# Eight modulation blocks a layer in 128-column pieces, issued ahead of the attention

## The chip, the cores and the metric

The kernel runs on one core of a Trainium2 chip. The metric is device time of one launch in microseconds (us). Matrix products run on TensorE (PE), which has two clock levels, 1.2 and 2.4 GHz; the profile gives the granted clock as a share of the higher one. VectorE (DVE), ScalarE (ACT) and GpSimd (POOL) do the rest. Each engine executes its own instructions in the order in which the build put them. Most loads and stores are issued from SP's queue, some from POOL's and ACT's.

## What is computed

One step of a two-layer trunk over 512 latent and 128 context tokens of 1024 channels. The parts that matter here:

```
for each layer l:
  m = silu(cond) @ w_mod[l] + b_mod[l]        # cond: latent c and context c_ctx; 6 * 1024 columns
  shift1, scale1, gate1, shift2, scale2, gate2 = six slices of m
  h = rms(x) * (1 + scale1) + shift1
  z = h @ w_in                                # columns for scan, queries, keys/values, gMLP
  y_a = two-way diagonal scan (16 groups, 64 complex states), GLU
  y_b = attention, 8 heads, queries and keys out of compressed vectors
  y_c = gMLP over chunks of 128 tokens
  x = x + gate1 * (concat(rms(y_a), rms(y_b), rms(y_c)) * g) @ w_out
  h = rms(x) * (1 + scale2) + shift2
  x = x + gate2 * (silu(conv3(h @ up_gate)) * conv3(h @ up_value)) @ w_down
```

Both condition vectors together are two rows, so the modulation is a product of two rows with a 1024 x 6144 matrix: 24 MB of weights a layer for little arithmetic.

## The kernel before

The activations lie transposed, channels on the partitions, 642 token columns in two halves. Products with large weights are made of three single-pass matmuls of high and low parts (`mm3`, lines 139 to 143); the parts come from `wload` (line 120), which loads 512 KB into one of three shared "raw" buffers, copies it to the high part on ACT and subtracts on DVE (`split`, line 115).

The 12 modulation blocks of 512 columns of a layer are made by the generator `mod_blocks` (line 230). Blocks 0 to 3 (shift1, scale1) come before the layer; blocks 4 to 11 are needed from the output projection on (`update`, line 1490, and the second norm). One step of the generator loads two of the eight k-tiles of a block (256 rows of 512 columns, runs of 2 KB) into a raw buffer on SP's queue (line 256) and issues two matmuls (line 260): the stationary operand is `sT`, 32 columns for a k-tile, the moving one 512 columns of float32, and the output lies in one of four groups of 32 partitions, k modulo 4. After four steps ACT copies the bank to `modev`, and with the next block's first step four transposes, a DVE reduce over the four groups, an add of the bias and at times a third operation give the columns (`finish`, line 235). The bank comes from the pool `pz` (two banks, tag "z"), which the attention uses for its transposes. One layer's generator of blocks 4 to 11 has 33 steps.

`mixers` (line 830) receives that generator as `fill`. Its order in the code: scan inputs and token-major parts of `w_in`, gMLP; in layer 0 then the scan tables of four quarters (`ssm_tables`, line 529, stores on SP's queue) and the scans (`ssm_quarter`, line 697, whose loads of tables are on POOL's queue); in layer 1 the scans come earlier, their tables having been made before. Then the compressed queries and keys (three column tiles of `w_in`, two halves each, `in_half` at line 854), keys and values (`w_ukv`, line 1019), queries (`w_uq`, line 1037). Five steps of `fill` are issued there, at line 1057. Then `attention` (line 1182): the context's own attention, and four passes of two heads each. `maxima` (line 1232) is a generator with a step for each query tile, and a step of `fill` is issued after each: eight in the context part, then eight in each of the passes 0 to 2 as far as there are any; what is left is issued at line 1420.

The build schedules ahead: it walks the instructions with an estimate of their times and priorities that follow the order of the code, gives out the buffers of a tag as they come free, and fixes the order on each engine. So an instruction may stand in its engine's queue before or after its neighbours in the code, but at run time each engine is in order.

PSUM in this part: two banks of `pz`, two of the pool `pa` (tag "a"; scores, statistics, token tiles) and two pairs of `pb`.

Of the kernel before, what the change touches and what calls it, by code (L numbers as in the profile page):

```python
# [10 lines left out]
F32 = mybir.dt.float32  # L11
# [17 lines left out]
NS = 82           # scan slots per row  # L29
# [18 lines left out]
class Trunk:  # L48
# [17 lines left out]
    def banks(self, pairs):  # L66
        """PSUM of one phase: six banks, as four single ones or two pairs of them."""
# [30 lines left out]
    def rsqrt(self, v, n):  # L98
        """v: [128, n] tile -> tile of 1/sqrt(v)."""
# [15 lines left out]
    def split(self, raw, hi, lo):  # L115
        """hi + lo == raw, each short enough for one float32r pass."""
        self.nc.scalar.copy(hi, raw)  # L117
        self.nc.vector.tensor_tensor(lo, raw, hi.bitcast(F32), op=OP.subtract)  # L118

    def wload(self, src, shape, pool=None, tags=("whi", "wlo"), bufs=5, into=None):  # L120
        """src: DRAM AP [128, a, b] (a*b <= 1024), or a list of (first index in a, AP)
        -> (hi, lo) views of that shape."""
        a, b = shape
        raw = self.wp.tile([128, 1024], F32, name=self.uid("raw"), tag="raw", bufs=3)
# [41 lines left out]
    def params(self, l):  # L166
        """Vectors of layer l with their index on the partitions."""
# [48 lines left out]
    def cond(self):  # L216
        """silu of both condition vectors, as 32-column stationary blocks."""
# [12 lines left out]
    def mod_blocks(self, l, blocks):  # L230
        """Blocks of 512 columns of the modulation of layer l; a generator of four steps a
        block and a last one."""
        nc = self.nc

        def finish(b, ev):
            pt = self.pz("modt")
            for i in range(4):
                self.tr(pt[:, i * 128:(i + 1) * 128], ev[:, i * 128:(i + 1) * 128])
            red = self.smt([128, 4, 2], "modred")
            nc.vector.tensor_reduce(  # L240
                red, pt.rearrange("p (i q r) -> p i r q", i=4, q=4)[:, :, 0:2, :],
                axis=AX.X, op=OP.add)
            m = self.mod[l][:, 4 * b:4 * b + 4, :]
            bias = self.prm[l][:, 4 * b:4 * b + 4]
            nc.vector.tensor_tensor(m, red, bc(bias[:, :, None], [128, 4, 2]), op=OP.add)
            if b // 2 in (1, 4):
                nc.vector.tensor_scalar(m, m, 1.0, None, op0=OP.add)

        last = None
        for b in blocks:  # L250
            src = self.I["w_mod"][l, :, b * 512:(b + 1) * 512].rearrange("(k p) n -> p k n", p=128)
            ps = self.pz("mod")
            for kp in range(4):
                raw = self.wp.tile([128, 1024], F32, name=self.uid("raw"), tag="raw", bufs=3)
# [16 lines left out]

    def modcol(self, l, i, k, c):
        return self.mod[l][:, i * 8 + k, c:c + 1]

    # ---------------------------------------------------------------- residual in and out
    def load_x(self):
# [3 lines left out]
        for tt in range(5):  # L280
            raw = self.wp.tile([128, 1024], F32, name=self.uid("raw"), tag="raw", bufs=3)
# [9 lines left out]
    def store_x(self, tiles):  # L291
        nc, O = self.nc, self.O
        for tt in tiles:
            o = self.wp.tile([128, 1024], F32, name=self.uid("xo"), tag="raw", bufs=3)
# [25 lines left out]
    def norm_stats(self, pool, lo, hi):  # L320
        """1 / rms of the columns lo .. hi, for bcast."""
# [39 lines left out]
    def bcast(self, pool, r, cols, *outs):  # L361
        """r: [128 tokens, n]; PSUM [128, 128] at column cols[i] of outs (512 columns each)
# [1385 lines left out]
```

## Time and profile before

| | us |
|---|---|
| runs shown, median (lowest to highest) | 1854.93 (1848.2 to 1855.78) |
| profiled execution, span | 1844.3 |
| PE busy in it | 1712.1 |
| DVE, ACT, POOL busy in it | 1153.7, 680.5, 265.3 |

The span runs from the first to the last instruction of one profiled execution. Busy times of an engine are unions over its instructions; matmuls are pipelined and overlap in the records. A float32 matmul leaves two records. A stretch below is given in us from the span's start.

### The profile page before, as it was taken

The page shows a single profiled execution, that of the slowest core. Times are in us where ns is not written, and L with a number is a line of the kernel's source. Part 1 is how long each engine was busy: PE and PEld are TensorE (multiplying, and loading weights), DVE is VectorE, ACT ScalarE, POOL GpSimd, SP SyncE. Part 2 cuts the span into 40 slices and gives each one's busy share as a digit, 9 for nine tenths or more (in the row PEclk, how much of TensorE's full clock was granted, in tenths as well). Part 3 has the DMA queues.
Part 4 walks back from the last instruction along what each step waited for, and adds up shares of the span by engine and source line. Part 5 has one row for each costly group of instructions (what it writes and reads, how often), then busy time and mean ns, then how long its engine had stood idle before and what let it go on. Part 6 is the DMA issues. An engine that isn't in the chain of part 4 may idle for free.

```text
span 1844.3 us, 28301 instructions
## 1 busy us (share of the span) xinstructions
PE 1712.1 (93%) x10864; PEld 1497.3 (81%) x10864; DVE 1153.7 (63%) x2461; ACT 680.5 (37%) x1210; POOL 265.3 (14%) x720
## 2 busy tenths in 40 slices
PE   6777889999999999999999988999989999999998
PEld 2665754559799899999998875455979999999998
DVE  5867784667764546466567578566777464655564
ACT  3342453532451414234244355353335132332241
POOL 3920300000024040439000120000000000000000
PEclk7886989999999999999999978999989999999999
DMA  7464534402433424134121633440222131321221
GB/s 222 135 163 123 140 110 159 138 1 69 126 119 100 151 65 126 54 98 125 54 89 66 159 107 105 156 141 1 69 69 92 32 107 44 94 82 45 81 81 58
DMA packets 201895, 182.44 MB, mean 99 GB/s; under 512 B 33438, under 2 KB 162780, under 8 KB 201760
## 3 DMA queue, kind: packets, MB, share of 16 engines
q1 hardware_dynamic: 182224, 163.57, 29.3%
q0 software_dynamic: 5104, 14.62, 2.7%
q10 hardware_dynamic: 14432, 2.44, 0.7%
q8 instruction: 86, 1.41, 0.3%
q14 instruction: 49, 0.40, 0.1%
HBM read 161.94 MB, written 18.64 MB: 98 GB/s over the span
## 4 chain that ended last, share of the span: by engine, by line
PE 74%; DVE 9%; DMA 8%; ACT 4%; POOL 3%; issue 2%; ACTq 0%; SPq 0%; DVEq 0%; POOLq 0%
PE up L141 11%; PE up L143 11%; PE up L142 11%; PE dn L142 5%; PE dn L141 5%; PE dn L143 5%; PE mod L260 4%; DMA raw<-w_mod 3%; PE o L1278 3%; PE wo L141 1%; PE wo L143 1%; PE wo L142 1%; PE s L1258 1%; PE mx L1239 1%; PE win L141 1%
## 5 line engine op out<-in xcount | busy, mean ns | idle before, releaser
L141 PE MATMUL up<-hh,whi 128*128 128x322 f32 x1408 | 436.5, 315 | 9.5 <-ACT hh L356 8.7
L142 PE MATMUL up<-hl,whi 128*128 128x322 f32 x1408 | 439.6, 313 | 2.1 <-DVE hl L357 1.9
L143 PE MATMUL up<-hh,wlo 128*128 128x322 f32 x1408 | 440.6, 314 | 0.4 <-DVE wlo L118 0.4
L141 PEld LDWEIGHTS up<-hh,whi 128*128 128x128 f32 x1408 | 266.2, 191 | 22.3 <-issue 11.0
L142 PEld LDWEIGHTS up<-hl,whi 128*128 128x128 f32 x1408 | 268.5, 191 | 2.9 <-DVE hl L357 2.9
L143 PEld LDWEIGHTS up<-hh,wlo 128*128 128x128 f32 x1408 | 267.9, 190 | 1.7 <-issue 1.0
L118 DVE TENSOR_TENSOR wlo<-raw,whi 128x1024 fp32r<-128x1024 f32 (+1 forms) x116 | 143.5, 1240 | 142.1 <-ACT whi L117 133.4
L142 PE MATMUL dn<-glo,dh 128*128 128x322 f32 (+1 forms) x704 | 217.7, 311 | 0.0
L143 PE MATMUL dn<-gh,dl 128*128 128x322 f32 (+1 forms) x704 | 217.4, 310 | 0.0
L141 PE MATMUL dn<-gh,dh 128*128 128x322 f32 (+1 forms) x704 | 208.8, 310 | 0.1
L1492 DVE SCALAR_TENSOR_TENSOR xT<-dn,mod,xT 128x320 f32<-128x320 f32 (+2 forms) x288 | 112.1, 435 | 129.9 <-PE dn L143 129.7
L117 ACT CAST whi<-raw 128x1024 fp32r<-128x1024 f32 (+1 forms) x116 | 120.4, 1041 | 157.1 <-PE up L142 63.9
L1523 ACT ACTIVATE cv<-up,prm,cw 128x321 f32<-128x321 f32 x88 | 54.2, 620 | 247.0 <-PE up L143 243.3
L143 PEld LDWEIGHTS dn<-gh,dl 128*128 128x128 f32 x704 | 132.9, 189 | 0.0
L142 PEld LDWEIGHTS dn<-glo,dh 128*128 128x128 f32 x704 | 132.7, 188 | 0.0
L141 PEld LDWEIGHTS dn<-gh,dh 128*128 128x128 f32 x704 | 130.3, 189 | 0.6 <-ACT gh L117 0.6
L260 PE MATMUL mod<-raw,sT 128*32 128x512 f32 x384 | 93.9, 672 | 20.1 <-DMA raw<-w_mod 17.2
L1524 DVE SCALAR_TENSOR_TENSOR cv<-up,cw,cv 128x320 f32<-128x320 f32 x88 | 48.3, 549 | 73.2 <-ACT cv L1523 73.0
L118 DVE TENSOR_TENSOR dl<-raw,dh 128x1024 fp32r<-128x1024 f32 x44 | 56.6, 1286 | 35.3 <-ACT dh L117 35.2
L1241 DVE TENSOR_REDUCE nml<-mx 128x1 f32<-128x640 f32 x64 | 51.1, 818 | 26.3 <-PE mx L1239 26.0
L117 ACT CAST dh<-raw 128x1024 fp32r<-128x1024 f32 x44 | 46.2, 1049 | 48.3 <-DMA raw<-ffn_w_down 44.9
L141 PE MATMUL wo<-yh,whi 128*128 128x322 f32 (+1 forms) x192 | 59.9, 317 | 1.8 <-ACT yh L117 1.0
(468 smaller groups left out, 3316.0 us busy)
## 6 DMA issues: line engine op xcount, KB each, us to landing
raw<-w_mod SPq DMA_DIRECT2D x96, 512.0 KB, 4.0
raw<-ffn_w_up SPq DMA_DIRECT2D x88, 512.0 KB, 4.0
raw<-ffn_w_down SPq DMA_DIRECT2D x44, 512.0 KB, 3.3
raw<-w_in SPq DMA_DIRECT2D x10, 512.0 KB, 4.8
WEd<-we SPq DMA_DIRECT2D x16, 256.0 KB, 2.1
Qd<-Q SPq DMA_DIRECT2D x32, 128.0 KB, 1.9
we<-WEd POOLq DMA_DIRECT2D x8, 512.0 KB, 4.1
qt<-Qd POOLq DMA_DIRECT2D x8, 512.0 KB, 5.0
```

The lines of the kernel that those rows point to most:

```text
L117: self.nc.scalar.copy(hi, raw)
L118: self.nc.vector.tensor_tensor(lo, raw, hi.bitcast(F32), op=OP.subtract)
L141: mm(ps, wh, xh, start=start, stop=False)
L142: mm(ps, wh, xl, start=False, stop=False)
L143: mm(ps, wl, xh, start=False, stop=stop)
L260: nc.tensor.matmul(ps[c:c + 32, :], self.sT[:, k, :], rv[:, j, :], start=k < 4, stop=k >= 4)
L1239: mm(pb[:, o, :320], qh[i][:96, tt * 128:(tt + 1) * 128], kh[i][:96, o * 320:(o + 1) * 320], start=True, stop=True)
L1241: V.tensor_reduce(nm[:, tt:tt + 1], pb[:, :, :320], axis=AX.XY, op=OP.max, negate=True)
L1278: mm(pb[i * 64:(i + 1) * 64, 0], Vt[:, kt, 2 * p + i], Ps[i][kt], start=kt == 0, stop=kt == 4)
L1492: self.nc.vector.scalar_tensor_tensor(self.xT[:, m, a:b], po[:, a - lo:b - lo], self.modcol(l, gi, m, c), self.xT[:, m, a:b], op0=OP.mult, ...
L1523: A.activation(z[:, 0:321], po[:, 0:321], AF.Identity, bias=b, scale=c1)
L1524: V.scalar_tensor_tensor(z[:, 1:321], po[:, 0:320], c0, z[:, 1:321], op0=OP.mult, op1=OP.add)
```

## The change

`mod_fill` takes the place of `mod_blocks` for blocks 4 to 11. One step loads all eight k-tiles of 128 columns (128 columns make runs of 512 B) into one raw buffer, issues eight matmuls of 128 columns, and ACT copies these 128 columns to `modev`; the fourth step of a block also does the transposes and the reduce at once. Banks come from `pa`. There are 32 steps a layer. They are issued two after the gMLP, two after each quarter of the scan tables (layer 0 only), two after each of six halves of the compressed projections, four after the key norms, and one after each of five query tiles: 31 in layer 0 and 23 in layer 1. The rest is issued by the loops of the attention, which are unchanged. `RAW` is 3, as before, and the loops over `range(0)` issue nothing. Comments and document strings are gone from the file, which has no effect.

```diff
     def mod_blocks(self, l, blocks):
...
+    def mod_fill(self, l, blocks):
+        nc = self.nc
+        def finish(b, ev):
+            pt = self.pa("modt")
+            for i in range(4):
+                self.tr(pt[:, i * 128:(i + 1) * 128], ev[:, i * 128:(i + 1) * 128])
+            self.mod_out(l, b, pt)
+        for b in blocks:
+            ev = self.smt([128, 512], "modev", bufs=1)
+            for i in range(4):
+                raw = self.wp.tile([128, 1024], F32, name=self.uid("raw"), tag="raw", bufs=RAW)
+                rv = raw.rearrange("p (k n) -> p k n", k=KT)
+                c = b * 512 + i * 128
+                nc.sync.dma_start(out=rv, in_=self.I["w_mod"][l, :, c:c + 128]
+                                  .rearrange("(k p) n -> p k n", p=128))
+                ps = self.pa("mod")
+                for k in range(KT):
+                    r = (k % 4) * 32
+                    nc.tensor.matmul(ps[r:r + 32, :128], self.sT[:, k, :], rv[:, k, :],
+                                     start=k < 4, stop=k >= 4)
+                nc.scalar.copy(ev[:, i * 128:(i + 1) * 128], ps[:, :128])
+                if i == 3:
+                    finish(b, ev)
+                yield
+    def mod_out(self, l, b, pt):      # reduce, bias, + 1: as in finish of mod_blocks
...
         self.gmlp(l, win, v, ssv, sq, yc, ssc)
+        for _ in range(2):
+            next(fill, None)
...
                 self.ssm_tables(0, q, tb, V)
+                for _ in range(2):
+                    next(fill, None)
...
                 in_half(m, w, s, put_c)
+                for _ in range(2):
+                    next(fill, None)
...
         self.key_norms(pt, ks, sc, ms, krn, kg)
+        for _ in range(4):
+            next(fill, None)
...
             V.tensor_reduce(ms[:, tt * 8:tt * 8 + 8], s2, axis=AX.X, op=OP.add)
+            for _ in range(1):
+                next(fill, None)
...
         self.query_norms(l, pt, qs, sc, ms, tab, [0, 1, 2, 3])
-        for _ in range(5):
-            next(fill, None)
...
-                fh, fl, second = self.mixers(l, M, n1, N, hh, hl, self.mod_blocks(l, range(4, 12)))
+                fh, fl, second = self.mixers(l, M, n1, N, hh, hl, self.mod_fill(l, range(4, 12)))
```

## Rows read from the trace of the kernel before

**Rows 1.** The page: busy us, share of the span and instructions of each engine.

```profile
PE 1712.1 (93%) x10864; PEld 1497.3 (81%) x10864; DVE 1153.7 (63%) x2461; ACT 680.5 (37%) x1210; POOL 265.3 (14%) x720
```

**Rows 2.** Busy time by stretch, layer 0 ahead of the attention; last: clock, DMA share, GB/s.

```profile
core 0: us, PE busy (x) PEld busy (x) DVE busy (x) ACT busy (x) POOL busy (x), PEclk, DMA share, GB/s
100.00:180.00 80.00, 54.68 (x418) 47.28 (x417) 54.95 (x161) 29.39 (x87) 7.77 (x31) 0.75 0.54 142
180.00:251.00 71.00, 61.53 (x394) 53.77 (x393) 58.05 (x147) 36.24 (x65) 15.57 (x43) 0.92 0.40 115
```

**Rows 3.** Busy time by stretch, layer 0: context attention (two), passes 0 to 2; columns above.

```profile
251.40:274.00 22.60, 17.27 (x93) 9.78 (x93) 15.62 (x38) 11.42 (x22) 3.27 (x6) 0.85 0.58 188
274.00:291.50 17.50, 15.94 (x81) 6.89 (x82) 8.92 (x15) 3.09 (x9) 0.00 (x0) 0.90 0.56 181
291.50:316.50 25.00, 24.86 (x117) 11.53 (x115) 12.76 (x30) 12.05 (x25) 0.00 (x0) 1.00 0.38 119
316.50:345.90 29.40, 27.74 (x139) 13.12 (x138) 15.60 (x27) 11.83 (x22) 0.00 (x0) 1.00 0.46 149
345.90:376.70 30.80, 28.68 (x134) 15.17 (x134) 23.35 (x38) 15.43 (x28) 0.24 (x2) 0.94 0.32 103
```

**Rows 4.** The same stretches, line 260 alone: PE, PEld; then its records from 230 to 460.

```profile
251.40:274.00 22.60, 7.45 (x32) 1.15 (x32) 0.85 0.58 188
274.00:291.50 17.50, 7.29 (x28) 1.22 (x28) 0.90 0.56 181
291.50:316.50 25.00, 5.26 (x20) 1.01 (x20) 1.00 0.38 119
316.50:345.90 29.40, 6.13 (x32) 0.98 (x32) 1.00 0.46 149
345.90:376.70 30.80, 3.72 (x16) 0.45 (x16) 0.94 0.32 103
...
L260 PE MATMUL mod<-raw,sT x128: 592/593/1062, 251.5 to 352.3; 128*32 128x512 f32 x128
```

**Rows 5.** Tile modt alone (the transposes), sum over 251.4 to 420 us.

```profile
sum 168.60, PE 5.13 PEld 3.48 DVE 1.49; mean PE 0.73 PEld 0.50 DVE 0.21
```

**Rows 6.** PE's waits: total us, times, longest; 251 to 355, then 1114 to 1235 us.

```profile
PE mod L260 <- DMA raw<-w_mod: 6.3, 4, 2.3
...
PE mod L260 <- DMA raw<-w_mod: 4.7, 4, 2.3
```

**Rows 7.** Busy time by stretch, layer 1: scans and projections, query norms; columns as rows 2.

```profile
1042.00:1114.00 72.00, 61.77 (x385) 54.33 (x384) 51.83 (x132) 34.15 (x75) 16.34 (x44) 0.83 0.37 107
1114.00:1152.00 38.00, 30.03 (x164) 21.53 (x162) 32.32 (x80) 20.20 (x32) 3.42 (x6) 0.87 0.39 126
```

**Rows 8.** Line 260 alone in layer 1, sum over 1020 to 1253.4 us.

```profile
sum 233.40, PE 27.58 PEld 4.50; mean PE 3.94 PEld 0.64
```

**Rows 9.** Timeline of PE: start, duration, line, operation, shapes, records in one row.

```profile
322.44 1.05 PE L260 MATMUL mod<-raw,sT 128*32 128x512 f32 x4 [1.01 <-DMA raw<-w_mod]
...
317.39 1.06 PE L260 MATMUL mod<-raw,sT 128*32 128x512 f32 x8
...
333.86 1.91 PE L260 MATMUL mod<-raw,sT 128*32 128x512 f32 x12
...
204.31 0.78 PE L713 MATMUL e<-U,we 128*64 128x81 f32 x16
...
177.20 1.35 PE L713 MATMUL e<-U,we 128*64 128x81 f32 x16 [0.34 <-ACT E L717]
```

**Rows 10.** Timeline of ACT: a copy of 128 columns out of PSUM.

```profile
289.26 0.27 ACT L1199 COPY yB<-co 128x128 f32<-128x128 f32 x1 [0.82 <-PE co L1334]
```

**Rows 11.** Loads: count, KB each, median us to landing; 274 to 291.5 us, then all.

```profile
raw<-w_mod SPq DMA_DIRECT2D x6, 512.0 KB, 3.9
...
raw<-ffn_w_up SPq DMA_DIRECT2D x88, 512.0 KB, 4.0
```

**Rows 12.** SP's waits, 180 to 260 us: issue of line 256 for PE; total, times, longest.

```profile
SPq L256 <- PE mod L260: 23.8, 3, 21.5
```

More of the change, by code (lines that the diff above doesn't have):

```diff
@@ L28 @@
 SCALE = 1.0 / math.sqrt(96.0)
+RAW = 3
 NS = 82
@@ L253, in mod_blocks @@
             for kp in range(4):
-                raw = self.wp.tile([128, 1024], F32, name=self.uid("raw"), tag="raw", bufs=3)
+                raw = self.wp.tile([128, 1024], F32, name=self.uid("raw"), tag="raw", bufs=RAW)
                 rv = raw.rearrange("p (a b) -> p a b", a=2)
@@ L270, in mod_blocks @@
         yield
+    def mod_fill(self, l, blocks):
[4 more added lines that the diff above has]
+                self.tr(pt[:, i * 128:(i + 1) * 128], ev[:, i * 128:(i + 1) * 128])
+            self.mod_out(l, b, pt)
+        for b in blocks:
+            ev = self.smt([128, 512], "modev", bufs=1)
+            for i in range(4):
+                raw = self.wp.tile([128, 1024], F32, name=self.uid("raw"), tag="raw", bufs=RAW)
+                rv = raw.rearrange("p (k n) -> p k n", k=KT)
[12 more added lines that the diff above has]
+    def mod_out(self, l, b, pt):
+        nc = self.nc
+        red = self.smt([128, 4, 2], "modred")
+        nc.vector.tensor_reduce(
+            red, pt.rearrange("p (i q r) -> p i r q", i=4, q=4)[:, :, 0:2, :],
+            axis=AX.X, op=OP.add)
+        m = self.mod[l][:, 4 * b:4 * b + 4, :]
+        bias = self.prm[l][:, 4 * b:4 * b + 4]
+        nc.vector.tensor_tensor(m, red, bc(bias[:, :, None], [128, 4, 2]), op=OP.add)
+        if b // 2 in (1, 4):
+            nc.vector.tensor_scalar(m, m, 1.0, None, op0=OP.add)
     def modcol(self, l, i, k, c):
@@ L293, in store_x @@
         for tt in tiles:
-            o = self.wp.tile([128, 1024], F32, name=self.uid("xo"), tag="raw", bufs=3)
+            o = self.wp.tile([128, 1024], F32, name=self.uid("xo"), tag="raw", bufs=RAW)
             dst = O["y_sample"][0, tt * 128:(tt + 1) * 128] if tt < 4 else O["y_prompt"][0]
@@ L914, in mixers @@
         wt = token_load(640, 288)
+        for _ in range(0):
+            next(fill, None)
         for tt in range(2):
             put_ku(tt, token_tile(tt, wt, 288))
+            for _ in range(0):
+                next(fill, None)
         in_half(0, w0, 1, put_u)
@@ L923, in scans @@
                 self.ssm_quarter(l, q, ssm, tables or self.ssm_load(l, q, ssm), U, st, hq)
+                for _ in range(0):
+                    next(fill, None)
                 tables = None
@@ L931, in mixers @@
             put_ku(tt, token_tile(tt, wt, 288))
+            for _ in range(0):
+                next(fill, None)
         nc.sync.dma_start(out=self.O["new_krope"][0, l], in_=kra[:, 5, :])
@@ L940, in mixers @@
             A.activation(sq, po, AF.Square, accum_out=ssv[:, tt:tt + 1])
+            for _ in range(0):
+                next(fill, None)
         self.gmlp(l, win, v, ssv, sq, yc, ssc)
+        for _ in range(2):
+            next(fill, None)
         win_ctx.close()
@@ L945, in mixers @@
                 self.ssm_tables(0, q, tb, V)
+                for _ in range(2):
+                    next(fill, None)
             tb_ctx.close()
@@ L985, in mixers @@
                 in_half(m, w, s, put_c)
+                for _ in range(2):
+                    next(fill, None)
         V.tensor_tensor(sqq, sqq, sq2, op=OP.add)
@@ L1036, in mixers @@
         self.key_norms(pt, ks, sc, ms, krn, kg)
+        for _ in range(4):
+            next(fill, None)
         wq = [self.wload(I["w_uq"][l, k * 128:(k + 1) * 128].rearrange("p (a n) -> p a n", a=1),
@@ L1053, in mixers @@
             V.tensor_reduce(ms[:, tt * 8:tt * 8 + 8], s2, axis=AX.X, op=OP.add)
+            for _ in range(1):
+                next(fill, None)
             if tt == 4:
```

18 lines of the change are left out of this document (4 added, 14 removed).

## The prediction

> **What bounds the kernel now.** I first read the page's busy shares: TensorE (PE) is busy for 1712.1 of the 1844.3 us and no other engine passes 63% [rows 1], so time is won by taking PE work away or by filling PE's idle time. I then cut layer 0 into stages, each with its own limit. Ahead of the attention PE idles: 25.3 us of the 80 us in which the scan tables are computed, 9.5 us of the 71 us of scans and projections, where VectorE (DVE) has 58.05 us of work [rows 2]. Inside the attention PE idles little: 0.1 to 5.3 us in each of five stretches [rows 3]. The modulation matmuls of line 260 lie in these five stretches alone and take 7.45 + 7.29 + 5.26 + 6.13 + 3.72 = 29.85 us of PE [rows 4]; their transposes take 5.13 us [rows 5]. All eight blocks of the layer (128 records, two a matmul) run between 251.5 and 352.3 us [rows 4], the five steps that the code places ahead of the attention too. Last come the waits: PE stood 6.3 us at modulation loads in layer 0, 4.7 us in layer 1 [rows 6]. In layer 1 PE idles 10.2 of 72 us ahead of the attention and 8.0 of 38 us in the stretch of query norms, where DVE has 32.32 us [rows 7].
>
> **The change: what leaves the attention.** Of the 32 steps a layer, layer 0 keeps one inside the attention and layer 1 nine; 31 and 23 go ahead of it. I take layer 0's five stretches one by one [rows 3, 4], and ask what is late next.
> - 251.4 to 274: PE without line 260 has 9.8 us, DVE 15.6; DVE is the next limit, and with the gaps between its dependent steps I put 17.5 for 22.6: 5 saved.
> - 274 to 291.5: PE 8.7, DVE 8.9, mostly maxima that now follow each other: 11 for 17.5, 6.5 saved.
> - 291.5 to 316.5: PE 19.6, DVE 12.8; still PE: 5 saved.
> - 316.5 to 345.9: PE 21.6 less some 1.3 of transposes, DVE 15.6: 22 for 29.4, 7.5 saved, a wait of 1 us among it.
> - 345.9 to 376.7: PE 25 less 1.8, DVE 23.35; both limits fall together: 26 for 30.8, 5 saved.
>
> That is 29, less one for the step that stays: **28 us**. The most would be all of 29.85 + 5.13 + 6.3 = 41; the least I allow is half of it, 20, if the cover that modulation gave to DVE's maxima is missed everywhere. In layer 1 the same work is 27.58 [rows 8] + 5.1 + 4.7 = 37 us; nine steps stay, at the price below 8 us, and of the remaining 29 the same share (28 of 41) gives **20 us** (13 to 27).
>
> **What a moved step costs PE.** A step becomes eight matmuls of 128 columns on the four 32-column groups of the array, where it was two of 512. No row shows that form, so I bound it. Two old matmuls side by side (x4: each is two records) take 1.05 us, four 1.06, six 1.91 [rows 9]: the groups work at the same time, a layer of 512 columns costs 0.85 us and the start some 0.2. Two layers of 128 columns are then 2 x 0.21 + 0.2 = 0.62 us. The scans' eight matmuls of 81 columns on two groups (x16) are the nearest row in count: 0.78 us at the full clock, 1.35 at the half [rows 9]. I take 0.7 (0.62 to 1.35), near the lower end since most of these stages runs at the full clock [rows 2, 7]. A block's four transposes stay at 5.13 / 8 = 0.64.
>
> On this the Trainium skill (TensorEngine Tiling, Key Properties) speaks against the change: it says that changing the tiling mode drains TensorE, and finer steps change it more often. The rows hold the 0.2 us start, which contains such a drain if there is one. If a switch cost nothing, a step would take 0.42, the 54 moved steps 11 us less, and the sum below would be -33; by the rows it is -22.
>
> **Where those steps land.**
> - Layer 0, tables: ten steps, 10 x 0.7 + 2.5 x 0.64 = 8.6 us, into 25.3 us of idle PE [rows 2]. Costed at nothing; uncovered it would be 8.6.
> - Layer 0, scans and projections: 21 steps, 14.7 + 3.4 = 18 us, into a stage with 9.5 us idle [rows 2]. PE runs in order, so half of the idle at most is filled: 18 - 4.7 = 13. The clock there is granted at 0.92 [rows 2], so some 16% of the stretch runs at the lower of the two levels; PE kept busier may win back a little. I take **+12** (3 to 25).
> - Layer 1, two steps in an early stage and 21 in scans, projections, keys and queries: 23 x 0.7 + 5.75 x 0.64 = 19.8 us against 10.2 idle [rows 7]: 19.8 - 5 = 15, less a little for a granted clock of 0.83, plus 2 for loads that meet the scan tables' loads. **+14** (3 to 30).
> - ScalarE: four copies of 128 columns at 0.27 [rows 10] for each block's single one, at most 1.1 us x 8 a layer. It has 36.24 us of work in 71 [rows 2]; costed at nothing, and 4 us a layer if it were not covered.
> - DVE: the same reduce, add and scalar step as before, at another place: nothing.
> - PSUM: the new steps take the two "a" banks, the old ones held one of two "z" banks over four steps. The attention's transposes get that bank back; nothing counted.
>
> **The loads.** Every step still issues one load of 512 KB on SP's queue, now in rows of 512 B. A load in that form (ffn_w_up) lands in 4.0 us, modulation loads of the old form in 3.9 [rows 11]; the size of the rows costs nothing there. They pass SP's queue of scan-table stores, scan loads and projection weights. A load waits until one of three "raw" buffers is free, and all that is queued behind it on SP waits too: SP stood 23.8 us at such waits between 180 and 260 us, 21.5 of it at one [rows 12], and behind that one only modulation and a constant were queued. After the change the stores of tables, for which POOL's loads of the scans wait, and w_in, w_ukv and w_uq stand behind. A late weight load is held up by the steps ahead of it in the ring; this is the second rival, and 2 us of it are in the sum.
>
> **The sum**: -28 - 20 + 12 + 14 = -22 us. Against the profiled execution the span goes from 1844.3 to 1822. The median of the runs shown, 1854.93, lies 10.6 above that span; I leave this as it is and predict 1854.93 - 22 = **1833 us**.
>
> **The rivals.**
> - *The steps hide.* They go wholly into idle PE and lift its clock in the projections. Layer 0 pays 18 - 9.5 = 8.5, of which the clock returns about 5; layer 1 pays 19.8 - 10.2 = 9.6, of which a clock of 0.83, a third of 72 us at the half level, could return all. Cost 4 to 6 in all: -48 + 6 = -42, **1813 us**. For it: idle time in both stages and the low granted clock [rows 2, 7]. Against it: PE takes its instructions in order, and most idle moments there are waits of an in-order queue, not free slots.
> - *The ring becomes the bound (slower).* While modulation ran nearly alone, six loads took 17.5 us (274 to 291.5), 2.9 us each [rows 3, 11], the ring waiting for PE and PE for the ring. With two steps behind every half of w_in, a weight load is issued up to two such slots late (5.8 us), and its own 4 us and its split follow. Five loads a layer (two of w_in, w_ukv, two of w_uq) at 6.5 us each are 32 us a layer, 64 in place of the 26 above: -48 + 64 = +16, **1871 us**. The change loses from the point where a load is delayed on the path by 48 / 10 = 4.8 us. Against it: the scans' DVE work, 58.05 and 51.83 us in those stages [rows 2, 7], runs meanwhile and covers part.
> - *The steps don't leave.* The build plans each engine's order ahead, and in the kernel before it pushed the five early steps into the attention. If buffers are late it does so again, and only the better packing of the column groups is won: some -7, **1848 us**. Against it: the new steps come before most of the projection in program order.
>
> **How the numbers follow.** Forecast 0.48, hiding 0.20, ring 0.20, steps that stay 0.12. The forecast's own range is 1822 to 1846: attention savings of 35 to 60 in all and costs of 18 to 45, the ends not falling together. For 8 in 10 I go down to 1808, five below the hiding case, and up to 1864, which takes in the steps that stay and a mild form of the ring, and leaves out its full price. A measurement of this kernel can tell about 0.5% from no change, 9.3 us: faster is below 1845.7, slower above 1864.2. Faster: nearly all of the forecast and all of hiding, 0.64. Same: the steps that stay and the edges of forecast and ring, 0.20. Slower: most of the ring, 0.16.
>
> **What would show it.** Modulation matmuls (128 columns) mainly at 110 to 250 us and 1040 to 1115 us, each step 0.6 to 0.8 us of PE; the attention of layer 0 from its start to the end of the third pass near 98 us in place of 125; scans and projections of layer 0 near 83 us in place of 71; no wait of PE at modulation loads in the later heads. A wrong prediction would show as waits of PE at weight splits behind w_in, w_ukv or w_uq loads, or of POOL's table loads at late stores (ring), as modulation still among the heads' maxima (steps that stay), or as projections no longer than before at a higher clock (hiding).

## The result, and the profile after

The kernel after takes 1880.01 us (median; 1871.73 to 1884.34) beside 1851.57 us for the kernel before on the same chip: a ratio of 1.0147 with a 95% interval of [1.0114, 1.018]. The forecast was 1833, with a range of 1808 to 1864. The time went the way of the rival with the ring of buffers, which was priced at 1871.

The spans of the two profiled executions differ by more than the medians: 1880.2 - 1844.3 = 35.9 us against 28.4. The profiled execution of before lay some 7 us under its median, so every difference of spans below is some 7 to 12 us higher than that of the medians. The verdicts go by the medians, the places by the spans.

First the page of after: the busy row, the group of the new matmuls (count, busy us, mean ns, idle time ahead of them), and the loads.

```profile
PE 1722.9 (92%) x11632; PEld 1525.7 (81%) x11632; DVE 1155.5 (61%) x2461; ACT 686.4 (37%) x1258; POOL 259.1 (14%) x720
...
L287 PE MATMUL mod<-raw,sT 128*32 128x128 f32 x1024 | 49.1, 317 | 25.0 <-DMA raw<-w_mod 15.4
...
raw<-w_mod SPq DMA_DIRECT2D x96, 512.0 KB, 4.8
```

PE's work has hardly changed (1712.1 before [rows 1]), so 36 us of span are 25 us more of idle PE and 11 more of busy PE. A step is 49.1 / 64 = 0.77 us. Now layer 0 by stretch: tables, scans and projections, then the attention as in [rows 3]; last the granted clock, the DMA share and GB/s.

```profile
core 0: us, PE busy (x) PEld busy (x) DVE busy (x) ACT busy (x) POOL busy (x), PEclk, DMA share, GB/s
100.00:180.00 80.00, 54.82 (x510) 43.86 (x510) 46.83 (x145) 27.33 (x86) 5.49 (x22) 0.74 0.73 190
180.00:283.40 103.40, 88.00 (x821) 72.59 (x820) 69.83 (x175) 46.85 (x98) 15.47 (x52) 0.92 0.71 201
283.40:306.00 22.60, 15.81 (x87) 12.85 (x86) 19.86 (x48) 11.33 (x21) 3.27 (x6) 0.70 0.19 64
306.00:316.50 10.50, 10.14 (x53) 6.46 (x52) 8.41 (x22) 3.69 (x9) 0.00 (x0) 0.84 0.00 0
316.50:336.50 20.00, 19.62 (x90) 9.50 (x91) 11.22 (x17) 10.24 (x23) 0.00 (x0) 1.00 0.00 1
336.50:359.40 22.90, 21.35 (x97) 11.35 (x98) 14.83 (x22) 10.80 (x21) 0.00 (x0) 1.00 0.00 1
359.40:390.10 30.70, 26.49 (x105) 15.20 (x106) 20.53 (x29) 12.16 (x24) 0.24 (x2) 0.83 0.00 1
```

Scans and projections take 103.4 us where they took 71 [rows 2], and DVE did less in the first 80 us than before (46.83 for 54.95): the tables too were late; the first scan matmul starts at 176.3 us where it started at 165.4. The five stretches of attention take 106.7 us for 125.3. The same stretches with line 287 alone show that the steps did move: 11 of them (176 records, 16 a step) among the tables, 20 in the next stretch, one after that.

```profile
100.00:180.00 80.00, 9.87 (x176) 5.75 (x176) 0.74 0.73 190
180.00:283.40 103.40, 14.12 (x320) 8.30 (x320) 0.92 0.71 201
283.40:306.00 22.60, 1.08 (x16) 0.60 (x16) 0.70 0.19 64
```

Next when SP issued the projection weights of layer 0 (start us, us, engine, line, load): five rows of before (six loads), then six of after.

```profile
130.96 1.21 SPq L134 DMA_DIRECT2D raw<-w_in  x2
135.67 0.38 SPq L134 DMA_DIRECT2D raw<-w_in  x1
153.88 0.34 SPq L134 DMA_DIRECT2D raw<-w_ukv  x1
155.02 0.33 SPq L134 DMA_DIRECT2D raw<-w_uq  x1
...
186.39 0.35 SPq L134 DMA_DIRECT2D raw<-w_uq  x1
```

```profile
169.77 0.45 SPq L135 DMA_DIRECT2D raw<-w_in  x1
187.10 0.43 SPq L135 DMA_DIRECT2D raw<-w_in  x1
203.59 0.37 SPq L135 DMA_DIRECT2D raw<-w_in  x1
219.62 1.29 SPq L135 DMA_DIRECT2D raw<-w_ukv  x1
243.85 0.35 SPq L135 DMA_DIRECT2D raw<-w_uq  x1
255.14 0.38 SPq L135 DMA_DIRECT2D raw<-w_uq  x1
```

Before, five of the six were issued while the tables were computed; after, each follows the modulation steps ahead of it, 39 to 89 us later than its like. SP's waits (total us, times, longest) say at what it stood in the meantime, in layer 0 (100 to 285 us) and in layer 1 (1030 to 1190).

```profile
SPq L282 <- PE mod L287: 31.1, 13, 7.4
...
SPq L135 <- PE mod L287: 6.1, 4, 2.7
```

```profile
SPq L282 <- PE mod L287: 50.8, 18, 16.8
```

Line 282 issues a modulation load. It waits until PE has done a step that holds one of the three raw buffers, and PE comes to that step only after the scan matmuls ahead of it in its own order. Of waits of this kind before had the 23.8 of [rows 12], with next to nothing queued behind the longest. The total of SP's waits doesn't tell the two apart: for raw buffers that PE, DVE or a transfer still held, lines 256 and 134 stood 51 us in before (100 to 253 us), lines 282 and 135 stood 54 us in after (100 to 285). My reading is that the difference lies in what stands behind the waits. Nor does PE stand long at the late weights. Of its waits in after (100 to 285 us) these two alone are for their splits:

```profile
PE win L144 <- DVE wlo L119: 0.7, 1, 0.7
...
PE win L142 <- ACT whi L118: 0.5, 1, 0.5
```

The account of the whole span, laid at the first transpose `ctr` and the last row sum `rs` of each layer's attention. The last two columns are experiments told below: e3 is after without the moved blocks' loads, e12 the fastest kernel.

| us of span | before | after | e3 | e12 | predicted change | after | e3 | e12 |
|---|---|---|---|---|---|---|---|---|
| to the attention of layer 0 | 253.3 | 285.4 | 261.7 | 259.5 | +12 | +32.1 | +8.4 | +6.2 |
| attention, layer 0 | 157.3 | 139.8 | 141.0 | 143.1 | -28 | -17.5 | -16.3 | -14.2 |
| from there to the attention of layer 1 | 726.2 | 747.5 | 733.6 | 732.6 | +14 | +21.3 | +7.4 | +6.4 |
| attention, layer 1 | 152.8 | 150.0 | 144.0 | 140.6 | -20 | -2.8 | -8.8 | -12.2 |
| the rest | 554.7 | 557.5 | 550.3 | 551.4 | 0 | +2.8 | -4.4 | -3.3 |
| sum | 1844.3 | 1880.2 | 1830.6 | 1827.2 | -22 | +35.9 | -13.7 | -17.1 |

Two steps failed by about the same amount: the projections cost 53 us in place of 26, and the attention gave 20 in place of 48.

### The profile page after: what moved, and what is told of

Same layout as the page of the kernel before. It is cut to its first block, busy times and chain, and to the rows that moved or that the text cites. A ratio compares the mean times of both kernels' runs of the same rounds, so it can differ in the third digit from the quotient of the medians.

```text
span 1880.2 us, 29931 instructions
## 1 busy us (share of the span) xinstructions
PE 1722.9 (92%) x11632; PEld 1525.7 (81%) x11632; DVE 1155.5 (61%) x2461; ACT 686.4 (37%) x1258; POOL 259.1 (14%) x720
## 4 chain that ended last, share of the span: by engine, by line
PE 73%; DMA 9%; DVE 9%; ACT 4%; POOL 3%; issue 2%; SPq 0%; ACTq 0%; DVEq 0%; POOLq 0%
PE up L142 11%; PE up L144 11%; PE up L143 11%; PE dn L143 5%; PE dn L144 5%; PE dn L142 5%; DMA raw<-w_mod 3%; PE o L1330 2%; PE wo L142 2%; PE wo L144 1%; PE wo L143 1%; PE mod L253 1%; PE mod L287 1%; PE s L1310 1%; PE mx L1291 1%
## 5 line engine op out<-in xcount | busy, mean ns | idle before, releaser
L119 DVE TENSOR_TENSOR dl<-raw,dh 128x1024 fp32r<-128x1024 f32 x44 | 57.4, 1304 | 46.1 <-ACT dh L118 45.6
L287 PE MATMUL mod<-raw,sT 128*32 128x128 f32 x1024 | 49.1, 317 | 25.0 <-DMA raw<-w_mod 15.4
L287 PEld LDWEIGHTS mod<-raw,sT 128*32 128x32 f32 x1024 | 29.2, 123 | 43.4 <-issue 14.9
```

Of the source, the lines that this page charges most:

```text
L287: nc.tensor.matmul(ps[r:r + 32, :128], self.sT[:, k, :], rv[:, k, :], start=k < 4, stop=k >= 4)
```

## The experiments

Theory: three raw buffers are shared by all weight loads, SP issues in order and PE works in order, so a modulation load that waits for a buffer holds up what comes behind it. Rivals: the new form of the step, the bytes themselves, and the tables' stores in particular. All ratios are to the kernel before on the same chip.

**e1, the new form at the old places.** The counts of steps at the new places are zero and the five steps ahead of the attention stand again.

```
-        for _ in range(2):      # all six new places
+        for _ in range(0):
+        for _ in range(5):      # ahead of the attention, as before
+            next(fill, None)
```

> The new 128-column steps at the old places: five after the query norms, the rest among the heads' maxima. Four theories of why the changed kernel takes 1880 us and not 1852. Form (the finer steps themselves cost: 16 records, an ACT copy and a bank each, transposes right behind the copy): 1870 or more, a ratio to the kernel before of 1.01 or more. Ring (the projections' weight loads and the tables' stores wait behind modulation loads for a buffer and on SP's queue), bandwidth (17 MB of loads more in the stages ahead of the attention slow the transfers there) and PE (the moved matmuls lengthen stages with little idle PE): all of them need the new places, so 1838 to 1855, ratio 0.992 to 1.002.

Measured: 1859.56 us, 1.0031 [1.0003, 1.0059]. The form alone wins nothing and costs perhaps 6 us.

**e2, the old form at the new places.** `mod_blocks` (512 columns, four steps a block) is called where after calls `mod_fill`.

```
-self.mod_fill(l, range(4, 12))
+self.mod_blocks(l, range(4, 12))
```

> The old 512-column steps (33 of them) at the new places. Form: most of the loss goes, 1850 to 1860. Ring, bandwidth and PE: the loss stays, 1872 to 1890, a ratio to the kernel before of 1.011 to 1.02; PE would make it a little worse than the changed kernel since an old step takes 1 us of PE when it stands alone, ring and bandwidth would not.

Measured: 1963.33 us, 1.0589 [1.056, 1.0618]. No theory had expected that; e15 comes back to it.

**e3, no loads.** The steps stand where after has them, but their matmuls read the identity and nothing is loaded.

```
-                raw = self.wp.tile(..., tag="raw", bufs=RAW)
-                nc.sync.dma_start(out=rv, in_=self.I["w_mod"]...)
-                    nc.tensor.matmul(..., rv[:, k, :], ...)
+                    nc.tensor.matmul(..., self.ident, ...)
```

> The changed kernel without the 64 loads of blocks 4 to 11: its modulation matmuls take the identity matrix that is there already as moving operand, so these modulation columns are not the reference's, and everything else is as in the changed kernel, with the same matmuls, copies, transposes and places. Ring and bandwidth: the whole loss goes and the attention's gain comes out, 1800 to 1832, ratio 0.97 to 0.99. PE and form: the engines' work is all there, 1865 to 1880, ratio 1.007 or more.

Measured: 1829.74 us, 0.9868 [0.9841, 0.9895]. All engine work of the change is still there, and the time is 50 us under after. The loads, or the buffers that they hold, cost 50 us; by the table 23.7 of it ahead of the first attention and 13.9 ahead of the second. From 100 us to the first attention, after and then e3 (columns as above):

```profile
100.00:285.40 185.40, 143.78 (x1332) 116.83 (x1331) 118.66 (x326) 74.18 (x184) 20.95 (x74) 0.84 0.71 196
```

```profile
100.00:261.70 161.70, 133.10 (x1328) 112.03 (x1328) 121.31 (x337) 75.53 (x188) 20.54 (x68) 0.91 0.48 128
```

Of the 23.7 us 13 are idle time of PE (41.6 us in after, 28.6 in e3), and 10.7 are the same matmuls taking longer at a lower granted clock (0.84 for 0.91).

**e4, weights first.** Each weight load of the projections is issued ahead of the steps that after puts before it.

```
-        for m in (4, 2, 3):
-            w = in_load(m)
+        w = in_load(4)
+        for m, m2 in ((4, 2), (2, 3), (3, None)):
+            w2 = in_load(m2) if m2 else self.wload(I["w_ukv"]...)
```

> The changed kernel with one thing moved: each weight load of the projections (w_in 2 and 3, w_ukv, the two of w_uq) stands in the code ahead of the modulation steps that it stood behind, so that it takes a buffer before them. Same loads, same bytes, same matmuls. Ring: most of the loss of the projections goes, 1845 to 1862, ratio 0.997 to 1.006, with w_in, w_ukv and w_uq issued 10 to 30 us earlier; the tables of layer 0, which are held up by stores behind modulation loads, stay as they are. Bandwidth and PE: 1872 to 1885, ratio 1.011 to 1.018.

Measured: 1874.58 us, 1.0131 [1.0081, 1.018]. A step or two further forward in program order gives back 5 of the 50, and the interval overlaps that of after. The loads did come earlier: those of `w_in` to `w_uq` were issued 4 to 26 us before their likes in after, as these two rows of e4 show beside the 219.62 and 243.85 above.

```profile
202.66 2.49 SPq L135 DMA_DIRECT2D raw<-w_ukv  x1
...
228.39 1.35 SPq L135 DMA_DIRECT2D raw<-w_uq  x2
```

Yet the key projection started at 234.6 us (230.4 in after), and PE stood 9.9 us at modulation loads (5.5 in after, 100 to 285 us). So lateness of the weights by itself isn't what costs 50 us; it seems that the steps lost in the ring what the weights gained.

**e5 and e9, a fourth raw buffer**, in after and, as a control, in before. To find the room, the accumulator of the norm's statistics has one buffer in place of two.

```
-RAW = 3
+RAW = 4
-        acc = pool.tile(..., tag="nacc", bufs=2)
+        acc = pool.tile(..., tag="nacc", bufs=1)
```

> The changed kernel with four raw buffers in place of three, all loads sharing them as before; room for it comes from one nacc buffer of the norms in place of two, which I put at nothing to 3 us. Without its modulation loads the changed kernel took 1830, so they cost 50 us; what is open is how. Ring (a load waits until PE or DVE has emptied a buffer, and every load and store behind it on SP waits too, so more buffers mean more loads under way): a good part comes back, 1850 to 1868. Bandwidth (the bytes meet the tables' and scans' transfers and slow them whatever waits for whom): 1874 to 1886.

> The control for four buffers: the kernel before with four raw buffers and one nacc buffer. If a fourth buffer gives something wherever loads are made (the up and down weights of the FFN too), it is 1825 to 1840 and says little of the change. If its gain with the change was the ring of the stages ahead of the attention: 1846 to 1858, no difference from the kernel before.

Measured: e5 1858.44 us, 1.0027 [1.0002, 1.0051]; e9 1852.54 us, 0.9991 [0.9976, 1.0005]. The same loads with one buffer more take 22 us less in after and nothing less in before. SP's waits for PE's steps at line 282 fall in layer 0 (100 to 285 us) from 31.1 to this:

```profile
SPq L135 <- PE mod L287: 17.2, 6, 4.9
SPq L282 <- PE mod L287: 14.1, 10, 5.1
```

**e6, the bytes beside the work.** The matmuls of e3, and the loads into one buffer of their own that nobody reads.

```
+                raw = self.wp.tile(..., tag="mraw", bufs=1)
-                    nc.tensor.matmul(..., rv[:, k, :], ...)
+                    nc.tensor.matmul(..., self.ident, ...)
```

> The matmuls of blocks 4 to 11 take the identity matrix as in the run without loads, but the 64 loads of 512 KB are issued all the same, at the same places on SP's queue, into one buffer of their own that nothing reads, so each waits only for the one before it and none for PE, and the weights have their three buffers to themselves. One nacc buffer less, as with four buffers. The modulation columns are not the reference's. Bandwidth: the bytes alone cost the 50 us, 1865 or more. Ring: 1828 to 1845, near the run without loads; in between, the two share it by the place of the result between 1830 and 1880.

Measured: 1888.67 us, 1.0202 [1.0165, 1.024]. The experiment doesn't separate what it was made for: with a single buffer each load waits on SP for the one before, and all other SP work behind it. Its SP waits from 100 to 300 us begin with

```profile
SPq L282 <- DMA raw<-w_mod: 99.5, 29, 6.5
```

Here the key weights weren't late (`w_ukv` was issued at 155.69 us, 153.88 in before), and yet the scans end at 260.2 us (225.1 in e3). So loads that no instruction waits for, that take no shared buffer, cost 59 us over e3 through the order of issue alone, or through their bytes; e10 is about the bytes.

**e10, an eighth of the bytes.** Each load brings one k-tile (64 KB), which all eight matmuls of the step read; count, places and buffers are those of after.

```
-                nc.sync.dma_start(out=rv, in_=self.I["w_mod"][l, :, c:c + 128]...)
+                nc.sync.dma_start(out=rv[:, 0], in_=self.I["w_mod"][l, 0:128, c:c + 128])
```

> The changed kernel with each modulation load cut to one of its eight k-tiles (64 KB in place of 512 KB), the eight matmuls all reading that one; same number of loads, places, buffers, waits and matmuls, wrong modulation columns. Ring by occupancy (a buffer is held from issue until PE has run the step, most of it the 4 to 6 us of landing plus PE's order): the landing falls to about 2 us and a part of the loss goes, 1848 to 1865. Transfer (bytes and landing are all of it): 1828 to 1842, as without loads. Order on SP alone (the waits for PE, whatever the size): 1868 to 1880.

Measured: 1867.61 us, 1.0075 [1.0054, 1.0096]. The landing from 100 to 285 us (count, KB, median us) falls from the first of these rows (after) to the second (e10), but only 12 of the 50 us come back. SP's wait at line 282 for PE is 33.2 us there, as in after: the buffers are held for as long, by PE's order and not by the transfer.

```profile
raw<-w_mod SPq DMA_DIRECT2D x32, 512.0 KB, 5.6
```

```profile
raw<-w_mod SPq DMA_DIRECT2D x32, 64.0 KB, 2.2
```

**e7, e11 and e8, fewer places.** e7 leaves out the steps among the tables, e11 those in the six halves of the projections; e8 leaves out both and those after the gMLP, so that nine steps a layer move, at the key norms and the query tiles.

```
e7   in ssm_tables:  range(2) -> range(0)
e11  in in_half:     range(2) -> range(0)
e8   both, and after gmlp: range(2) -> range(0)
```

> The changed kernel without the eight steps among the scan tables of layer 0; they go to where the generator's rest runs, among the maxima of the attention, as nine of layer 1 do already. In the changed kernel the first scan matmul of layer 0 came 11 us later than before. If stores of tables behind modulation loads, or slowed by them, are that delay and it stays to the end: 1866 to 1874, with the first scan matmul back near 165 us. If the stage has room to make it up later (the scans being paced by something else): 1876 to 1884.

> The changed kernel without the twelve steps in the compressed projections of w_in, which go among the maxima of the attention; the tables, the gMLP, key norms and queries keep theirs. Taking the table steps out gave back 7 us, taking those, the gMLP's and these out together 30. If w_in and w_ukv behind modulation are most of the loss: 1850 to 1862. If the loss is spread by the number of steps (12 of 54 places, both layers 24 of 54): 1864 to 1870.

> Only the nine steps after the key norms and the query tiles stay ahead of the attention, in both layers; none among the tables, after the gMLP or in the compressed projections. Ring: weight loads of w_in and w_ukv no longer stand behind modulation, only w_uq does: 1845 to 1860. Bandwidth: the scans' transfers are over by then, also 1845 to 1860. PE (the moved work itself) would give 1860 to 1870. If it is 1850 or less, a place with idle DMA queues is what the move needs.

Measured: e7 1873.05 us, 1.0124 [1.0087, 1.016]; e11 1870.0 us, 1.0083 [1.0057, 1.0109]; e8 1849.64 us, 0.9986 [0.9969, 1.0004]. Either place left out gives 7 to 10 us (e7's interval overlaps that of after); all of them 30. No single place is the fault. The sign that e7's expectation named didn't come: its first scan matmul starts at 175.4 us, hardly earlier than after's 176.3, though no step stands among the tables; in e8 it starts at 166.8. My reading, which no run shows by itself, is that the ring stays full while any stretch of in-order work lies between its steps.

**e12, nine steps and four buffers: the version that beats both.** e8 with the edit of e5.

> The version that the runs point to: only the nine steps at keys and queries ahead of the attention, with four raw buffers. If both effects add: 1832 to 1844, faster than the kernel before. If the fourth buffer only repaired the ring of the crowded stages, which this version does not have: 1846 to 1856.

Measured: 1825.73 us, 0.9845 [0.9824, 0.9866], 28.6 us under before and 54 under after. Nine steps a layer are now ahead of the attention (144 records in the first row) and 23 within it:

```profile
180.00:257.50 77.50, 6.48 (x144) 3.72 (x144) 0.91 0.61 164
257.50:368.00 110.50, 15.94 (x368) 10.04 (x368) 0.94 0.43 120
```

**e13, the same form and buffers at the old places.** e1 with the edit of e5. (What the expectation calls a rounding buffer is the accumulator of the norm's statistics.)

> All sixteen blocks stand at the places of the kernel before; the last eight are loaded and multiplied in the 128-column form of the kernel after, with four buffers for the loads instead of three and one rounding buffer instead of two. Theory (the ring): the places among the keys' and queries' projections were worth the 33.8 us by which e12 (1825.7) lies under e1 (1859.6), once the fourth buffer removed the waits; at the old places the fourth buffer has little to free, so 1850 to 1860. Rival (the fourth buffer alone makes the 128-column form good, wherever it stands): 1824 to 1838. Between them the two share it.

Measured: 1855.73 us, 1.0014 [0.9991, 1.0037]. The rival falls: form and buffers without the places give nothing, so the 30 us between e13 and e12 belong to the nine moved steps a layer.

**e14, a buffer of their own.** After with four buffers, one for the moved blocks, three for the other weights.

```
-                raw = self.wp.tile(..., tag="raw", bufs=RAW)
+                raw = self.wp.tile(..., tag="mraw", bufs=1)
```

> The kernel after with four buffers for 512 KB loads as in e5, but one of them is for the moved blocks alone and three are for the other weights. Theory (held buffers block the others' loads because SP issues in order): the moved loads now wait each for the four steps before them, on the same queue, so what stands behind them on SP still waits; between e5 and after or above, 1865 to 1890. Rival (what hurts is that the blocks take buffers out of the ring of the other weights): the weights have their three buffers again, 1835 to 1858.

Measured: 1978.2 us, 1.0679 [1.0647, 1.0711], above what either theory expected. Taking the modulation loads out of the shared ring is no cure: with the other weights' three buffers untouched, and one buffer for all modulation loads, the kernel is 98 us slower than after. SP's waits from 100 to 400 us, then PE's longest in total, then when SP issued the key weights:

```profile
SPq L282 <- DMA raw<-w_mod: 82.4, 23, 5.7
SPq L282 <- PE mod L287: 36.8, 27, 4.0
```

```profile
PE mod L287 <- DMA raw<-w_mod: 61.4, 19, 11.3
...
150.09 0.53 SPq L135 DMA_DIRECT2D raw<-w_ukv  x1
```

Every load now waits for the step before it, and PE for every load. The key weights aren't late here: they were issued as early as in before (153.88). But the key projection stands behind the steps in PE's order, and that is where the time goes, so this run doesn't decide between its two theories. The key projection starts at 296.6 us (230.4 in after), though the scans were done at 225.6 (246.9 in after):

```profile
L1077 PE MATMUL kv<-whi,ckh x12: 394/398/774, 296.6 to 309.0; 128*128 128x512 f32 x12
```

**e15, the old form with another bank.** e2 with its four-step accumulation in the PSUM buffers "pa" in place of "pz", which the projections use.

```
-            ps = self.pz("mod")
+            ps = self.pa("mod")
```

> The same as e2 (512-column blocks of the form before at the new places), except that the four steps of a block accumulate in the PSUM buffers of the attention instead of those that the projections use. Theory (in e2 the accumulating bank was held over four steps while the tables and projections wanted it): the excess over after goes, 1865 to 1890. Rival (the excess is the four 512-column matmuls per step and their loads): still 1940 to 1970.

Measured: 1927.93 us, 1.0412 [1.0365, 1.046], between the two expectations. Of the 83 us by which e2 lies over after, the bank is worth 35. The other 48 stay open: per step the old form loads and multiplies as much as the new one.

**e16, e17 and e18, another queue.** POOL issues the moved loads in place of SP: in after, in e5 and in e12.

```
-                nc.sync.dma_start(out=rv, in_=self.I["w_mod"][l, :, c:c + 128]
+                nc.gpsimd.dma_start(out=rv, in_=self.I["w_mod"][l, :, c:c + 128]
```

> The kernel after, three shared buffers, with the moved blocks' loads issued by POOL instead of SP. Theory (in-order issue on SP: table stores and weight loads stand behind a modulation load that waits for a buffer): these go ahead again, and most of the 50 us go that e3 gave back; POOL's own scan loads and table work may now stand behind, so 1835 to 1862. Rival (the sharing of three buffers alone is what costs, whichever queue issues): 1872 to 1890. Above that, POOL's queue blocks worse than SP's did.

> As e16 with four buffers and one accumulator of the norm's statistics, as in e5 (1858.4 on SP's queue). Theory (SP order): another gain of 10 to 25 over e5, 1833 to 1848. Rival (the buffers alone): as e5, 1852 to 1864.

> e12 (nine steps at keys and queries, four buffers, 1825.7) with the moved loads issued by POOL. In these stages POOL has little to do and SP stood at such loads for less. Theory: within 6 us of e12, 1820 to 1832. Rival (SP's order still costs in e12): 1805 to 1818. Against both: POOL's issue of the loads costs time of its own, 1835 to 1850.

Measured: e16 1879.38 us, 1.0132 [1.0102, 1.0163]; e17 1886.2 us, 1.0175 [1.0141, 1.0208]; e18 1844.99 us, 0.9956 [0.9937, 0.9976]. None is faster than its like on SP, and e17 and e18 are 28 and 19 us slower. In e18 the time lies in the attention, where 46 of its 64 steps stand: 152.2 us in either layer for 143.1 and 140.6 in e12, while the way to the first attention is 4 us shorter. In e16 SP no longer issues the moved loads, and yet its weight loads (line 135) stand for 52 us between 100 and 290 us, now for the shared buffers themselves; and each load takes POOL 0.89 us (last row: count, busy us, mean ns, idle time ahead):

```profile
SPq L135 <- DMA raw<-w_mod: 32.6, 2, 20.3
SPq L135 <- PE mod L287: 19.7, 6, 8.9
```

```profile
L282 POOL DMA_DIRECT2D raw<-w_mod x64 | 56.9, 890 | 181.3 <-PE mod L287 87.8
```

So taking the order on SP away is no cure while the buffers are shared (e16), and a single buffer of the loads' own is none either, as PE's steps then wait for each load (e14). e16 doesn't price the order on SP, though: since e18 shows that POOL's issue has a price of its own, a gain on SP of that size may be hidden in it. How the 50 us divide between ring and queue stays open; 12 of them go with the bytes (e10).

## Why the prediction was wrong

- **What bounds the kernel** was read rightly in the main: of the 36 us more of span 25 are idle time of PE, and 11 are busy time, though the matmuls of the moved blocks take 49.1 us for 57.4 before (29.85 + 27.58).
- **The price of a step** held: 0.77 us on average, at mixed clocks, for 0.7 (0.62 to 1.35); a step by itself took 0.64 or 1.08 us (at 187.80 and 189.35 us of after). The sentence on the Trainium skill (TensorEngine Tiling (Array Packing), Key Properties) can be answered only in part: a step took 0.64 us and not the 0.42 of a switch without cost, but no run shows a drain by itself, and there are no more steps than before (32 for 33 a layer). The -33 also took off 0.2 us a step where 0.7 to 0.42 is 0.28, which is 15 us and -37.
- **The steps leave the attention**: they did (one left in layer 0, nine in layer 1), so the rival in which they stay is out; and e1 shows that its -7 for a better packing was wrong as well.
- **Steps among tables and projections, 26 us**: right as far as the engines go. Without the loads (e3) these stretches grow by 8.4 + 7.4 = 15.8 us. With them they grow by 53.4. The prediction let the steps fill idle time of PE, all ten among the tables and a part of the others. In e3 they do: from 100 us to the first attention PE idles 28.6 us for 35.1 in before. In after it idles 41.6; the steps filled nothing and came on top. The step that failed is "2 us of it are in the sum": the loads cost these stretches 37.6 us. The prediction saw the ring, found the point from which it decides (4.8 us a load), and put against it that DVE's scan work runs meanwhile. That was the mistake: as I read the rows, the scan work doesn't cover the delay, it makes it. Loads wait for buffers, buffers for steps on PE, steps on PE for the scan matmuls ahead of them; so the weights of the projections came not two ring slots late but 39 to 89 us later than before, behind the scans instead of beside them. [Rows 12] had shown one wait of 21.5 us of just this kind. Which late transfer then costs what isn't shown: PE stood 1.2 us at splits of late weights, weights that came earlier won next to nothing (e4), and with weights as early as in before e6 and e14 were slower still. That the number of buffers weighs more than the bytes or one place is shown by e5 with e9 (22 us and nothing), e10 and e7, e11, e8.
- **The queue.** The Trainium skill (DMA: Bandwidth & Descriptors, Anatomy of one DMA — SWDGE (gpsimd) path) says, in its account of the path through GpSimd, that DMA engines wait on no semaphore and that the wait happens on the issuing sequencer before dispatch. The rows of SP show the same on SP's queue: 31.1 us in layer 0 in after, 99.5 in e6.
- **The attention, 48 us**: it gave 20.3, 25.1 without the loads, below the least that was allowed in both layers (20 and 13). Of layer 0's five stretches the three in the middle came out as predicted (10.5 us for 11, 20.0 for 20, 22.9 for 22), but the first stayed at 22.6 us where 17.5 was put, and the last at 30.7 for 26. In both the granted clock (a mean of its two levels, 2.4 GHz at 1.00 and 1.2 GHz at 0.50) fell: 0.70 for 0.85 and 0.83 for 0.94 [rows 3]. In the first the clock doesn't explain the time by itself. DVE has 19.86 us of work there (48 instructions) for 15.62 (38) before [rows 3]: two more pieces of the GLU, a pair of query products and a weight split now fall into this stretch, and the chain of work that ended last runs on DVE from 282.6 to 299.2 us, but for some 2 us on ScalarE. The prediction had named DVE as the next limit and counted on its old work. The rows below, the attention of each layer from `ctr` to `rs`, show what the clock is worth over the whole; first before, then after, then e12.

```profile
253.30:410.60 157.30, 143.41 (x686) 73.74 (x685) 96.32 (x175) 65.86 (x129) 3.52 (x8) 0.96 0.35 114
...
1136.80:1289.60 152.80, 139.52 (x660) 75.19 (x661) 95.38 (x174) 63.27 (x123) 0.24 (x2) 0.93 0.28 90
```

```profile
285.40:425.20 139.80, 124.43 (x560) 73.82 (x561) 94.98 (x166) 60.49 (x122) 3.52 (x8) 0.89 0.03 8
...
1172.70:1322.70 150.00, 131.23 (x702) 76.75 (x703) 97.62 (x169) 63.84 (x131) 0.24 (x2) 0.90 0.13 39
```

```profile
259.50:402.60 143.10, 130.71 (x929) 80.63 (x930) 96.83 (x174) 67.47 (x144) 3.52 (x8) 0.94 0.33 93
...
1135.20:1275.80 140.60, 129.13 (x929) 78.87 (x930) 95.40 (x172) 65.18 (x140) 0.24 (x2) 0.96 0.33 94
```

In layer 0 PE's other work, with line 287 taken off, is 124.43 - 1.08 = 123.4 us in after and 130.71 - 15.94 = 114.8 in e12: the same instructions, in e12 even with the transposes of five more blocks, cost 8.6 us more at a mean granted clock of 0.89 than at 0.94. In layer 1, e12 keeps 23 steps in the attention and is 9.4 us shorter there than after, which keeps nine, at 0.96 against 0.90; 6 of these us go with the loads, as e3 takes 144.0 with the same nine steps at 0.89. What PE did where the clock fell: in the first stretch it idled 6.8 of 22.6 us (5.3 before), and it now waits for DVE's maxima, which the steps had covered (layer 1, 1172 to 1323 us; before, no wait of this kind is among its first rows):

```profile
PE mx L1291 <- DVE nml L1293: 7.0, 6, 3.5
```

The prediction named this cover only for its lower bound. That the steps held the clock up is read from these rows and from e3 (141.0 us in layer 0 at 0.85); no run was made for it alone. The other runs bear it out for layer 0: 0.83 to 0.89 in the eleven kernels with one step or none in its attention, 0.90 (e7) and 0.91 (e11) with nine and thirteen, 0.92 to 0.96 in the seven with 23 or more. In layer 1 it holds less well: 0.90 with 27 steps (e1) and 0.91 with 23 (e8), but 0.92 with nine (e4).
- **The total of e3, 1829.7, is close to the forecast's 1833 by two misses that cancel in part**: by spans it is -13.7, its projections 10 us cheaper than put and its attention 23 us poorer.
- **Right on the other side**: of the rival's price of 1871 the mechanism held in so far as the loads and their buffers are what costs (e3, e5); that it goes through late weights isn't shown. Its size (64 us for both fronts) was near the 53.4 measured; what made the rest of the difference is the attention. Of its two signs one came weakly and one not: POOL's longest wait for a scan table (`Qd`) is 21.9 us for 16.9 before, and PE hardly waits at weight splits. The hiding rival put 4 to 6 us on both fronts; even e3, without the loads, pays 15.8.

## What to carry to other kernels

Ahead of moving a load into a busy stretch, count the buffers of its ring and ask, for each load, behind which work its buffer's last reader stands on its own engine; that whole distance, and not only the landing time, can delay everything queued behind it on the issuing queue. Move a little first: with a fourth buffer, nine steps a layer at a place next to their old one won 26 us in the attention at 6 us a layer ahead of it (e12), and with the other 36 of the 54 steps the same four buffers gave no gain at all (e5). Filler work between dependent steps of another engine is not all cost, as it may be what keeps the matmul clock granted.

## What the runs showed of the hardware

- A fourth load buffer was worth 22 us in after, 24 on top of nine moved steps (e8 to e12), and 0 in before (e9).
- The same load issued by POOL occupies it for 0.89 us; 64 of them, 56.9 us, made e12 19 us slower.
- Loads in rows of 512 B landed in 5.6 us (median of 32, 100 to 285 us) at 190 to 201 GB/s, and modulation loads of the old form in 3.9 while little else ran [rows 11]; yet an eighth of the bytes won only 12 of 50 us.
- The attention of layer 0 ran at a mean granted clock of 0.96 with all modulation in it, 0.94 with 23 of 32 steps, 0.89 with one; its other matmul work grew from 114.8 to 123.4 us between the last two. Over all runs that clock lay at 0.83 to 0.89 with one step or none and at 0.92 to 0.96 with 23 or more.
